# Conv + RWKV-7 + GLA trunk: two PSUM banks for the chain, three for small products, and a new order of the work around the chain

## The chip, the cores and the metric

The kernel runs on one core of a Trainium2 chip. The metric is the device time in microseconds. The kernel before took 1541.42, 1541.05 and 1535.45 us in three runs, median 1541.05.

## What is computed

A trunk of two layers over 128 context tokens and 512 noisy tokens (640 columns in the kernel), 1024 features, everything in float32. The first layer runs a short gated convolution and a bidirectional RWKV-7 recurrence on 16 heads of 64 side by side, the second layer bidirectional gated linear attention (GLA). The part that matters here is the recurrence of the first layer:

```python
u, gb, gc, zc, r, k, v, zw = jnp.split(h @ w_in, EVEN_SPLITS, axis=-1)
kk = heads(kf * k_k)
kk = kk / jnp.maximum(jnp.sqrt(jnp.sum(kk * kk, axis=-1, keepdims=True)), 1e-12)
def step(s, inp):                       # one token, state s of [value, key]
    r_t, w_t, k_t, kk_t, a_t, v_t = inp
    s_kk = jnp.einsum('zbhvk,zbhk->zbhv', s, kk_t)
    s = (s * w_t[..., None, :] - s_kk[..., :, None] * (kk_t * a_t)[..., None, :]
         + v_t[..., :, None] * k_t[..., None, :])
    return s, jnp.einsum('zbhvk,zbhk->zbhv', s, r_t)
```

## The kernel before

The recurrence is computed in chunks of 64 tokens: ten chunks in two directions d, for two heads at a time. Such a head pair is called hp (0 to 7). For each pair the products between the tokens of a chunk (the matrices G), the inverse of a triangular matrix made of them, and then a **chain** of eight steps are needed, in which the state X goes from chunk to chunk. The chain is serial, so its eight steps are cut into six **gaps** each, and the 48 gaps of a pair's **period** are filled with other work: the dense projections (blocks of 48 matmuls of 128x320, three products of split fp32r parts for each real one: r, v, k, zw of a pair and the units u, gc, gb, zc of the convolution), and **small work** that prepares the next pair.

The small work for pair hp+1 runs in period hp, in this order. `p_kb` scales the keys by the norms `rnb` (transposes into `prb`, VectorE product). `expand_all` makes the decayed operands ar and bk (VectorE and ScalarE, L733 to L766) and calls `pairs`, which forms the chunk products pG on TensorE and lets VectorE mask and evict them into G (L778). `inv_a` sends the diagonal blocks of G through DRAM (Ad) into the tile Ai, where a ladder of 60 VectorE operations inverts them (L845, L847), and back through DRAM (Td) into G. `inv_b` transposes them on VectorE (Tb, L868) and finishes the inverse with the products pT. `vrows`, `bonus`, `p_lr`, `p_kk` follow. `fin_b` and `fin_t` finish the pair before (normalised output oac, transposed into pgn, evicted by ScalarE into gn at L1061).

Orders are set in two ways. TensorE's instructions stay in the order in which the program writes them; this order comes from the class `Period`, which in each gap first runs the pieces of small work (`Work`) that are due by the table `PR`, and then as many pieces of dense work as a quota gives. On the other engines the scheduler goes by priorities: chain (CH) before evictions (EV), weight splits (SPL), preparation (PRE), finishing (FIN), background (BG). Each engine then runs its instructions strictly in the order written.

A chain step (`chain_step`) writes the products x and v into the bank pa; ScalarE copies them to rh (L958); two gaps; TensorE writes pu and adds to pa; ScalarE makes U from pa (L984); TensorE adds the products of U to pu; two gaps; VectorE makes the next state X from pu (L997). `bk_start` transposes the bk of the next step's chunks into the bank pbk, and ScalarE evicts them to bkt (L905). PSUM has eight banks: three for the dense blocks (psD), two in turn for small products (psM, function `pm`), and three for the chain (psC: pa, pu, pbk).

## Time and profile before

| What | us |
| --- | --- |
| Median of three runs | 1541.05 |
| The profiled execution | 1539.62 |
| its span | 1537.8 |
| setup, to the first dense matmul | 53.5 |
| preparation of pair 0 | 53.5 to 195.2 |
| periods 0 and 1 | 195.2 to 424.2 |
| periods 2 to 5, about 119.5 each | 424.2 to 902.5 |
| period 6 | 902.5 to 1014.5 |
| period 7, with the loads of the second layer | 1014.5 to 1141.2 |
| output projection and GLA layer | 1141.2 to 1537.8 |
| TensorE busy | 1362.7 (89%) |
| VectorE busy | 983.4 (64%) |
| ScalarE busy | 633.9 (41%) |
| GpSimd busy | 519.7 (34%) |

A stage starts where TensorE runs the first product of a pair's first chain step. Idle time of TensorE is listed by what released it: "pT <- DVE Tb" is time in which TensorE's next instruction writes pT and the last thing that it needed was VectorE's Tb. The granted clock tells at which share of its full speed TensorE was allowed to run; it has two levels, 1 (2.4 GHz) and 0.5 (1.2 GHz), and a mean between them is a mixture in time.

### The profile page before, as it was taken

The page shows a single profiled execution, that of the slowest core. Times are in us where ns is not written, and L with a number is a line of the kernel's source. Part 1 is how long each engine was busy: PE and PEld are TensorE (multiplying, and loading weights), DVE is VectorE, ACT ScalarE, POOL GpSimd, SP SyncE. Part 2 cuts the span into 40 slices and gives each one's busy share as a digit, 9 for nine tenths or more (in the row PEclk, how much of TensorE's full clock was granted, in tenths as well). Part 3 has the DMA queues.
Part 4 walks back from the last instruction along what each step waited for, and adds up shares of the span by engine and source line. Part 5 has one row for each costly group of instructions (what it writes and reads, how often), then busy time and mean ns, then how long its engine had stood idle before and what let it go on. Part 6 is the DMA issues. An engine that isn't in the chain of part 4 may idle for free. (4 is left out here: it accounts for less than half of the span.)

```text
span 1537.8 us, 34577 instructions
## 1 busy us (share of the span) xinstructions
PE 1362.7 (89%) x13495; PEld 1236.5 (80%) x13495; DVE 983.4 (64%) x2315; ACT 633.9 (41%) x1574; POOL 519.7 (34%) x675
## 2 busy tenths in 40 slices
PE   9689689589989989989998898789897999999997
PEld 4679678578878878878887887678887898999997
DVE  5285476486585595685675765766885668737554
ACT  4443253343443443443443353253235583444341
POOL 2333233123323232223323223144455534443332
PEclk9879899789989999999998998888998999999999
DMA  9012212112212212212212212236652332323233
GB/s 357 28 52 80 56 50 57 40 32 70 63 38 65 65 39 65 72 37 66 65 41 63 60 45 79 75 99 177 190 157 85 116 97 64 120 69 94 62 120 100
DMA packets 139636, 127.28 MB, mean 83 GB/s; under 512 B 54096, under 2 KB 121936, under 8 KB 139472
## 3 DMA queue, kind: packets, MB, share of 16 engines
q1 hardware_dynamic: 136912, 118.38, 25.9%
q0 software_dynamic: 2016, 6.16, 1.1%
...
q14 instruction: 58, 0.48, 0.1%
...
## 5 line engine op out<-in xcount | busy, mean ns | idle before, releaser
L130 PE MATMUL pG<-ar,bk 64*128 64x128 f32 x640 | 73.7, 336 | 39.5 <-ACT gn L1061 31.4
L847 DVE TENSOR_TENSOR Ai<-Ai 80x30 f32<-80x30 f32 (+14 forms) x240 | 100.6, 419 | 6.8
L845 DVE TENSOR_TENSOR Ai<-Ai 80x30 f32<-80x30 f32 (+14 forms) x240 | 94.6, 394 | 12.2 <-DMA Ai<-Ad 4.6
L130 PEld LDWEIGHTS pG<-ar,bk 64*128 64x128 f32 x640 | 56.3, 221 | 54.9 <-ACT gn L1061 33.7
L778 DVE TENSOR_TENSOR G<-pG,con 128x256 f32<-128x256 f32 (+1 forms) x128 | 57.8, 484 | 43.7 <-PE pG L130 42.9
L997 DVE SCALAR_TENSOR_TENSOR X<-pu,PC,XP 128x64 f32<-128x64 f32 x144 | 33.1, 274 | 62.6 <-POOL lo_zc L314 42.2
L228 DVE SCALAR_TENSOR_TENSOR gacc<-gw,cf,gacc 128x512 f32<-128x512 f32 x70 | 60.5, 909 | 11.9 <-DMA gw<-in_ada_dram 11.7
L952 POOL TENSOR_TENSOR XP<-X,PC 128x128 f32<-128x128 f32 (+2 forms) x56 | 29.1, 519 | 113.5 <-DVE X L997 80.8
L130 PE MATMUL pT<-Tb,G 32*32 32x32 f32 x640 | 17.5, 207 | 51.6 <-DVE Tb L868 51.6
L130 PEld LDWEIGHTS pT<-Tb,G 32*32 32x32 f32 x640 | 14.8, 121 | 55.4 <-issue 30.8
L677 DVE TENSOR_TENSOR_SCAN lw<-con,lw 128x320 f32<-128x320 f32 x32 | 28.8, 934 | 43.0 <-ACT lw L672 43.0
L314 POOL TENSOR_TENSOR lo_eoc<-wr_eoc,hi_eoc 128x256 fp32r<-128x256 f32 x48 | 44.3, 930 | 34.3 <-ACT hi_eoc L311 32.9
L130 PE MATMUL pd_r<-hi,hi_r 128*128 128x320 f32 x128 | 43.1, 337 | 11.5 <-ACT hi_r L311 11.5
L984 ACT ACTIVATE U<-pa 128x192 f32<-128x192 f32 (+1 forms) x64 | 19.3, 302 | 79.8 <-PE pa L130 78.8
L314 POOL TENSOR_TENSOR lo_gc<-wr_gc,hi_gc 128x256 fp32r<-128x256 f32 x32 | 25.9, 816 | 67.2 <-PE pd_r L130 43.5
L130 PE MATMUL pd_gc<-hi,lo_gc 128*128 128x320 f32 x128 | 47.8, 373 | 0.0
L1010 DVE SCALAR_TENSOR_TENSOR sz<-sz,pd_zw 128x320 f32<-128x320 f32 x16 | 7.7, 484 | 62.6 <-ACT sz L1009 62.6
L314 POOL TENSOR_TENSOR lo_gb<-wr_gb,hi_gb 128x256 fp32r<-128x256 f32 x32 | 26.3, 822 | 60.0 <-ACT hi_gb L311 59.6
L130 PE MATMUL pd_gc<-lo,hi_gc 128*128 128x320 f32 x128 | 45.8, 358 | 0.0
L130 PE MATMUL pd_gc<-hi,hi_gc 128*128 128x320 f32 x128 | 45.3, 354 | 0.0
L314 POOL TENSOR_TENSOR lo_zc<-wr_zc,hi_zc 128x256 fp32r<-128x256 f32 x32 | 23.8, 746 | 62.8 <-ACT hi_zc L311 61.8
L130 PE MATMUL pd_eoc<-hi,hi_eoc 128*128 128x320 f32 x128 | 44.4, 347 | 0.0
...
## 6 DMA issues: line engine op xcount, KB each, us to landing
...
```

Of the source, the lines that this page charges most:

```text
L130: tc.keep_in_program_order(T.matmul(*a, **kw))
L228: V.scalar_tensor_tensor(acc[j], w, c, acc[j], op0=ALU.mult, op1=ALU.add)
L314: le.tensor_tensor(lo, w, hi.bitcast(F32), op=ALU.subtract)
L677: V.tensor_tensor_scan(x, m, x, 0.0, op0=ALU.mult, op1=ALU.add)
L778: V.tensor_tensor(q["G"][h][:, d, c0 + a0:c0 + a0 + m], ps[h][:, 0:P * m].rearrange("p (c x) -> p c x", x=P), cc("mk", P, 256 * h + P * d) ...
L845: V.tensor_tensor(tt, Ai[:, 0:i, i:i + 1].to_broadcast([80, i, n]), Ai[:, i:i + 1, i + 1:].to_broadcast([80, i, n]), op=ALU.mult)
L847: V.tensor_tensor(Ai[:, 0:i, i + 1:], Ai[:, 0:i, i + 1:], tt, op=ALU.add)
L952: dict(V=V, G=G)[PR["xpc"]].tensor_tensor(XP[:, l0:nl], X[:, l0:nl], PC[:, s, l0:nl].unsqueeze(2).to_broadcast([P, nl - l0, 64]), op=ALU.mult)
L984: S.activation(U[:, 0:nl], pr[:, 0:nl], AF.Copy, scale=-1.0)
L997: V.scalar_tensor_tensor(Xn[:, l], po[:, 0, l], PC[:, s, l:l + 1], XP[:, l], op0=ALU.mult, op1=ALU.add)
L1010: V.scalar_tensor_tensor(sz[:, t], sz[:, t], 1.0, ps, op0=ALU.add, op1=ALU.mult)
```

## The change

- **Banks.** The chain holds pa and pu only. `bk_start` now stands after U, ahead of the products of U, and writes its transposes into columns 0 to 384 of pa, which U has just been read from. The bank pbk becomes the third in the turn of `pm`, from the end of the setup to the second layer's norm.
- **Chunk products in six units** of 4, 4 and 2 chunks for each direction, not eight of 3 and 2. A direction's four Ad transfers are issued as soon as its last unit is evicted; the layout of Ad and Td has the direction first.
- **Keys a period ahead.** `p_kb` of a pair runs at gaps 45 and 46 of the period before its preparation, not at gaps 0 to 2 of the preparation itself.
- **Order inside the gaps** (`Period`, "paired"): the first gap of each pair runs small work, then dense; the second dense, then small work. `inv_b` comes in two pieces, not four.
- **Priorities.** Small products' evictions run at the eviction priority (`evict`), `inv_a` just behind, `fin_s` behind that.
- **Table.** Convolution units after the change: 8 in the preparation of pair 0 (7 before), 4 in period 0 (1), 3 in each of periods 2 to 5 (4); one of the seven output blocks of period 7 moves behind the chain. The sum of the work stays. The expansion spreads over gaps 1 to 16 (5 to 14), `inv_a` is due at 17 (15), `inv_b` at 42 to 45 (40 to 44).
- **Weights.** The four weight blocks of the first dense block r0 are loaded and split during the setup.

The core of the diff follows; of the table it shows three entries. Left out are the eviction calls of the other small products, the allocation of PC, ar, bk and G (now in `expand_all`), the loop order of `inv_b`, and the planner's lines with the new pieces' numbers.

```diff
@@ table PR @@
- 'CN': [[1, 0, 0], [2, 1, 1], [2, 1, 1], [2, 1, 1], [2, 1, 1], [2, 1, 1], [2, 1, 1]],
+ 'CN': [[2, 1, 1], [2, 1, 1], [1, 1, 1], [1, 1, 1], [1, 1, 1], [1, 1, 1], [2, 1, 1]],
 ...
- 'ex': [5, 14],
- 'inv': 15,
+ 'ex': [1, 16],
+ 'inv': 17,
@@ -154,8 +159,22 @@
+    turn = [None]
     def pm(name):
+        if turn[0] is not None:
+            turn[0] += 1
+            if turn[0] % 3 == 2:
+                return psC.tile([P, 512], F32, tag="pbk", name=name)
         return psM.tile([P, 512], F32, tag="m", name=name)
+    def evict(f):
+        p = tc.cur_priority
+        prio(min(EV, p))
+        f()
+        prio(p)
@@ -523,6 +547,10 @@
+            prio(SPL)
+            for q in range(4):
+                ahead["r0", q] = weights(A["ew"][32], "r0", q)
+            prio(1)
@@ -559,6 +587,7 @@
+    turn[0] = 0
     st[0] = dict(k=et("k", "k0"), ok="k")
@@ -709,14 +739,8 @@
-            V.scalar_tensor_tensor(kk[:, u], k[:, u], pc("kk", hp), prb[:, 0:(t1 - t0) * P], op0=ALU.mult, op1=ALU.mult)
+            evict(lambda: V.scalar_tensor_tensor(kk[:, u], k[:, u], pc("kk", hp), prb[:, 0:(t1 - t0) * P], op0=ALU.mult, op1=ALU.mult))
@@ -765,34 +789,46 @@
-    def pairs(hp, d, c0, a0, m):
+    def pairs(hp, d, c0, m):
         q = st[hp]
-        bk, ar = q["bk"][:, d, c0:c0 + 5], q["ar"][:, d, c0:c0 + 5]
+        bk, ar = q["bk"][:, d, c0:c0 + m], q["ar"][:, d, c0:c0 + m]
+        ps = [pm(f"pG{hp}_{d}_{c0}_{h}") for h in range(2)]
         for i in range(m):
             for h in range(2):
-                mm(ps[h][:, P * i:P * i + P], bk[HS[h], a0 + i].rearrange("p a x -> p (a x)"),
-                   ar[HS[h], a0 + i].rearrange("p a x -> p (a x)"), start=True, stop=True)
-        for h in range(2):
-            V.tensor_tensor(q["G"][h][:, d, c0 + a0:c0 + a0 + m], ps[h][:, 0:P * m].rearrange("p (c x) -> p c x", x=P),
-                            cc("mk", P, 256 * h + P * d).unsqueeze(1).to_broadcast([P, m, P]), op=ALU.mult)
+                mm(ps[h][:, P * i:P * i + P], bk[HS[h], i].rearrange("p a x -> p (a x)"),
+                   ar[HS[h], i].rearrange("p a x -> p (a x)"), start=True, stop=True)
+        def ev():
+            for h in range(2):
+                V.tensor_tensor(q["G"][h][:, d, c0:c0 + m], ps[h][:, 0:P * m].rearrange("p (c x) -> p c x", x=P),
+                                cc("mk", P, 256 * h + P * d).unsqueeze(1).to_broadcast([P, m, P]), op=ALU.mult)
+        evict(ev)
 ...
-        quarters = [(d, c0) for d in range(2) for c0 in (0, 5)]
-        for x in quarters[:2]:
-            expand(hp, *x)
+        q = st[hp]
+        for c0 in (0, 5):
+            expand(hp, 0, c0)
-        for i, (d, c0) in enumerate(quarters):
-            pairs(hp, d, c0, 0, 3)
-            yield 520
-            pairs(hp, d, c0, 3, 2)
-            if i < 2:
-                expand(hp, *quarters[i + 2])
-            if i == 3:
-                st[hp]["ok"] += "g"
-            yield 520
+        for d in range(2):
+            for i, (c0, m) in enumerate(((0, 4), (4, 4), (8, 2))):
+                pairs(hp, d, c0, m)
+                if d == 0 and i < 2:
+                    expand(hp, 1, 5 * i)
+                if i == 2:
+                    for b in range(2):
+                        for h in range(2):
+                            r = 64 * (1 - h) + B * b
+                            nc.sync.dma_start(Ad[d, b, h].rearrange("c j t -> j c t"), st[hp]["G"][h][r:r + B, d, :, C + B * b:C + B * b + B])
+                    if d:
+                        st[hp]["ok"] += "g"
+                yield 210 * m
@@ -831,14 +870,9 @@
         Gt = st[hp]["G"]
-        for b in range(2):
-            for d in range(2):
-                for h in range(2):
-                    r = 64 * (1 - h) + B * b
-                    nc.sync.dma_start(Ad[b, d, h].rearrange("c j t -> j c t"), Gt[h][r:r + B, d, :, C + B * b:C + B * b + B])
-        nc.sync.dma_start(Ai, Ad.rearrange("b d h c j t -> (b d h c) j t"))
+        nc.sync.dma_start(Ai, Ad.rearrange("d b h c j t -> (d b h c) j t"))
         for i in range(1, B - 1):
@@ -891,13 +926,14 @@
-    def bk_start(hp, s):
+    def bk_start(hp, s, ta):
 ...
         q = st[hp]
-        pb = psC.tile([P, 3, P], F32, tag="pbk", name=f"pbk{hp}_{s}")
+        pb = ta[:, 0:384].rearrange("p (l x) -> p l x", x=P)
         for (l, d, c) in lanes:
             tr(pb[:, l], q["bk"][:, d, c].rearrange("p a x -> p (a x)"), ident)
@@ -926,12 +962,13 @@
+        ta, tu = (psC.tile([P, 512], F32, tag=t, name=f"{t}{hp}_{s}") for t in ("pa", "pu"))
+        pr = ta[:, 0:192].rearrange("p (l x) -> p l x", l=3)
+        po = tu[:, 0:384].rearrange("p (a l x) -> p a l x", a=2, l=3)
         if s == 0:
-            bk_start(hp, 0)
+            bk_start(hp, 0, ta)
-        pr = psC.tile([P, 3, 64], F32, tag="pa", name=f"pa{hp}_{s}")
-        po = psC.tile([P, 2, 3, 64], F32, tag="pu", name=f"pu{hp}_{s}")
@@ -988,6 +1024,7 @@
         def gu_mm(l, d, c, h):
             mm(po[HS[h], 1, l], Gt[h][HB[h], d, c, 0:C], U[HB[h], l], start=False, stop=l == nl - 1, skip_group_check=True)
+        bk_start(hp, s + 1, ta)
         each(bu_mm, upd)
         each(gu_mm, lanes)
@@ -1118,12 +1159,18 @@
-        def __call__(self):
+        def small(self):
             for m in self.misc:
                 m.upto(self.g)
-            self.credit += self.quota[self.g]
-            self.g += 1
-            if self.g == len(self.quota):
+        def __call__(self):
+            back = self.paired and self.g % 2
+            if not back:
+                self.small()
+            g = self.g
+            self.credit += self.quota[g]
+            if g + 1 == len(self.quota):
                 self.credit += 1e6
@@ -1132,6 +1179,9 @@
                     self.credit -= x
+            if back:
+                self.small()
+            self.g += 1
             prio(CH)
@@ -1226,17 +1276,19 @@
         if n < NHP:
-            misc += [Work(PRE, p_kb(n), 2, *PR["kb" + z], 270)]
+            if hp == 0:
+                misc += [Work(PRE, p_kb(1), 2, 0, 1, 270)]
             if hp == 0 and PR["lr1"]:
                 misc += [Work(PRE, p_lr(1), 9, *PR["lr1"], 270)]
-            misc += [Work(PRE, expand_all(n), 10, *PR["ex" + z], 540, (n, "r"))]
+            misc += [Work(PRE, expand_all(n), 8, *(PR["ex" + z] if hp else PR["ex0"]), 540, (n, "r"))]
+            iv = iv if hp else PR["inv0"]
 ...
             dense_ += [(FIN, p_z(hp)), *conv_next(c)]
@@ -1277,7 +1329,7 @@
         f.rest()
-        prio(FIN)
+        prio(EV + 600)
         run(fin_s(hp, 1 if hp == 7 else None))
@@ -1351,6 +1403,7 @@
     pss = psC.tile([P, 512], F32, tag="pa", name="pss1")
+    turn[0] = None
```

Three places show what moves. The first is TensorE in period 4, at the transposes pgn of pair 3's output between the chunk products pG of pair 5 (the last numbers tell tiles apart; pG5_0_0_3_0 is direction 0, chunks from 3 on, head 0). Before:

```order
L130 MATMUL pu4_1_8097<-U4_1_8253,G4_0_6456 64x64
L130 MATMUL pu4_1_8097<-U4_1_8253,G4_1_6457 64x64
L133 MATMUL pgn3_0_8267<-con_79,oac3_6074 128x128 x4
L130 MATMUL pG5_0_0_3_0_8276<-ar5_8009,bk5_8010 128x128
L130 MATMUL pG5_0_0_3_1_8277<-ar5_8009,bk5_8010 128x128
```

After:

```order
L135 MATMUL pd_v5_0_8481<-lo0_104,hi_v5_0_8459 128x320
L135 MATMUL pd_v5_0_8481<-hi0_103,lo_v5_0_8460 128x320
L138 MATMUL pgn3_0_8488<-con_79,oac3_6251 128x128 x4
L135 MATMUL pG5_1_4_0_8497<-ar5_8230,bk5_8231 128x128
L135 MATMUL pG5_1_4_1_8498<-ar5_8230,bk5_8231 128x128
```

Behind the transposes now comes the second unit of direction 1, not of direction 0, and a block of v ahead of them in place of the chain's products.

The second is VectorE in the same period, at the end of the ladder (Ai5), with the transposes Tb5 and the state X4_6 that the chain's next step reads. Before:

```order
L847 TENSOR_TENSOR Ai5_8529<-Ai5_8529 80x30
L1010 SCALAR_TENSOR_TENSOR sz4_9047<-sz4_9047,pd_zw4_0_9072 128x320
L997 SCALAR_TENSOR_TENSOR X4_6_9244<-pu4_6_9012,PC4_6453,XP4_6_9023 128x64 x3
L914 TENSOR_TENSOR oac4_7629<-pu4_6_9012,oac4_7629 128x2x64
L918 TENSOR_TENSOR oac4_7629<-pu4_6_9012,oac4_7629 128x64
L868 STREAM_TRANSPOSE Tb5_9153<-G5_0_8011 32x320
L868 STREAM_TRANSPOSE Tb5_9153<-G5_1_8012 32x320
```

After:

```order
L881 TENSOR_TENSOR Ai5_8592<-Ai5_8592 80x30
L1047 SCALAR_TENSOR_TENSOR sz4_9019<-sz4_9019,pd_zw4_0_9044 128x320
L900 STREAM_TRANSPOSE Tb5_9276<-G5_0_8232 32x320
L1034 SCALAR_TENSOR_TENSOR X4_6_9254<-pu4_6_9063,PC4_6772,XP4_6_9074 128x64 x3
L950 TENSOR_TENSOR oac4_7714<-pu4_6_9063,oac4_7714 128x2x64
L954 TENSOR_TENSOR oac4_7714<-pu4_6_9063,oac4_7714 128x64
L706 SCALAR_TENSOR_TENSOR lw6_9125<-con_79,lw6_9125 128x320
L900 STREAM_TRANSPOSE Tb5_9276<-G5_0_8232 32x320
L900 STREAM_TRANSPOSE Tb5_9276<-G5_1_8233 32x320
```

The first transpose has moved ahead of the state update, and scans of `p_lr` (lw6) stand between the others.

The third is TensorE at the start of period 4. Before, with the transposes in their own bank:

```order
L130 MATMUL pd_u5_1_7851<-hi0_103,lo_u5_3_7760 128x320
L133 MATMUL pbk4_0_7939<-con_79,bk4_6455 128x128 x3
L130 MATMUL pa4_0_7945<-X4_i_7626,ar4_6454 64x64 x4
L130 MATMUL pa4_0_7945<-V4_7316,G4_0_6456 64x64
L130 MATMUL pa4_0_7945<-V4_7316,G4_1_6457 64x64
```

After, in the bank pa4_0 itself:

```order
L135 MATMUL pd_gb5_1_7960<-hi0_103,lo_gb5_3_7761 128x320
L138 MATMUL pa4_0_8034<-con_79,bk4_6774 128x128 x3
L135 MATMUL pa4_0_8034<-X4_i_7711,ar4_6773 64x64 x4
L135 MATMUL pa4_0_8034<-V4_7359,G4_0_6775 64x64
L135 MATMUL pa4_0_8034<-V4_7359,G4_1_6776 64x64
```

The products of X4_i now write the bank that ScalarE reads the transposes from (bkt4_0).

## Rows read from the trace of the kernel before

**Rows 1.** The cores' answer: span, mean granted clock of TensorE (1 is full).

```profile
core 0: 1537.8 us, clock 0.932
```

**Rows 2.** Windows by stage: us, each engine's busy us (instructions), granted clock, DMA share, GB/s.

```profile
53.50:195.20 141.70, 111.70 (x841) 105.13 (x841) 81.54 (x186) 53.43 (x127) 48.72 (x61) 0.83 0.21 60
...
543.70:663.30 119.60, 106.97 (x1297) 96.20 (x1296) 78.89 (x208) 50.49 (x129) 36.51 (x51) 0.94 0.20 57
...
1141.20:1537.80 396.60, 365.37 (x2420) 351.69 (x2418) 241.05 (x521) 177.52 (x443) 161.50 (x206) 0.97 0.30 94
```

**Rows 3.** TensorE's waits, whole span: line, releaser, total us, times, longest us.

```profile
PE pT L130 <- DVE Tb L868: 51.6, 16, 13.1
PE pG L130 <- ACT gn L1061: 31.4, 12, 4.2
PE prb L133 <- DVE rnb L701: 15.3, 6, 3.8
PE pd_r L130 <- ACT hi_r L311: 11.5, 1, 11.5
PE pgn L133 <- DVE oac L1045: 10.6, 2, 9.6
PE pgn L133 <- DVE G L778: 6.5, 6, 1.2
PE pG L130 <- DVE G L778: 5.3, 3, 4.0
PE pa L130 <- DVE X L997: 4.0, 10, 1.1
```

**Rows 4.** Timeline around 568 us: start us, us, engine, what, idle before it.

```profile
568.13 0.66 PE L133 MATMUL pgn<-con,oac 128*128 128x128 f32 x4 [1.06 <-DVE G L778]
...
568.72 0.49 PE L130 MATMUL pG<-ar,bk 64*128 64x128 f32 x2
...
572.23 1.13 ACT L1061 ACTIVATE gn<-pgn,der 64x256 f32<-64x256 f32 x2
...
573.41 1.22 PE L130 MATMUL pG<-ar,bk 64*128 64x128 f32 x6 [4.20 <-ACT gn L1061]
```

**Rows 5.** Windows, TensorE alone, right after that wait: us, busy, granted clock.

```profile
569.58:579.82 10.24, 6.41 (x31) 0.50 0.15 50
```

**Rows 6.** Windows of the same period: expansion, and the inverse's ladder.

```profile
540.00:577.00 37.00, 29.37 (x343) 26.48 (x343) 33.66 (x95) 16.72 (x41) 12.16 (x16) 0.90 0.12 37
...
605.00:635.00 30.00, 29.79 (x338) 27.05 (x338) 28.03 (x74) 13.04 (x37) 10.22 (x16) 1.00 0.21 65
```

**Rows 7.** Timeline of VectorE: last eviction of G, ladder's ends, first transpose.

```profile
595.76 0.76 DVE L778 TENSOR_TENSOR G<-pG,con 128x256 f32<-128x256 f32 x2
...
605.01 0.18 DVE L845 TENSOR_TENSOR Ai<-Ai 80x30 f32<-80x30 f32 x1
...
634.76 0.21 DVE L847 TENSOR_TENSOR Ai<-Ai 80x30 f32<-80x30 f32 x1
...
639.56 2.21 DVE L868 STREAM_TRANSPOSE Tb<-G 32x320 f32<-32x320 f32 x4 [1.42 <-DMA G<-Td]
```

**Rows 8.** Groups by form, 543.7 to 663.3 us: VectorE's evictions of G.

```profile
L778 DVE TENSOR_TENSOR G<-pG,con 128x384 f32<-128x384 f32 x8 | 4.2, 551 | 4.4 <-PE pG L130 4.4
...
L778 DVE TENSOR_TENSOR G<-pG,con 128x256 f32<-128x256 f32 x8 | 3.1, 419 | 2.5 <-PE pG L130 2.4
```

**Rows 9.** The same view, TensorE: transposes for the state update.

```profile
L133 PE MATMUL pbk<-con,bk 128*128 128x128 f32 x19 | 4.0, 295 | 0.1
```

**Rows 10.** The same view, ScalarE: their eviction.

```profile
L905 ACT ACTIVATE bkt<-pbk 128x384 f32<-128x384 f32 x4 | 1.9, 485 | 0.3 <-PE pbk L133 0.3
```

**Rows 11.** Timeline of TensorE ahead of that transpose: dense products, then the chain's.

```profile
635.72 0.31 PE L130 MATMUL pd_zw<-hi,lo_zw 128*128 128x320 f32 x1
635.87 0.31 PE L130 MATMUL pd_zw<-hi,hi_zw 128*128 128x320 f32 x1
636.11 0.56 PE L130 MATMUL pu<-U,bkt 64*64 64x64 f32 x12
```

More of the change, by code (lines that the diff above doesn't have):

```diff
@@ L16 @@
  'pex': [4, 12],
+ 'ex0': [4, 15],
+ 'inv0': 16,
+ 'ib0': [44, 47],
+ 'lr0': [36, 43],
+ 'kk0': [42, 44],
  'pinv': 13,
@@ L27 @@
  'pinit': 30,
- 'ex': [5, 14],
- 'inv': 15,
- 'vr': 30,
- 'bo': [31, 33],
- 'lr': [36, 44],
- 'kk': [44, 47],
+ 'ex': [1, 16],
+ 'inv': 17,
+ 'vr': 26,
+ 'bo': [28, 30],
+ 'lr': [34, 41],
+ 'kk': [40, 42],
  'init': 40,
- 'fb': 7,
- 'ft': [10, 16],
- 'kb': [0, 2],
+ 'fb': 10,
+ 'ft': [13, 16],
+ 'kb': [45, 46],
  'al': 1.0,
@@ L67 @@
  'sh': 0.25,
- 'ex6': [5, 14],
- 'inv6': 15,
- 'vr6': 30,
- 'bo6': [31, 33],
+ 'ex6': [1, 16],
+ 'inv6': 17,
+ 'vr6': 26,
+ 'bo6': [28, 30],
  'init6': 43,
- 'fb6': 8,
- 'ft6': [11, 16],
- 'kb6': [0, 2],
+ 'fb6': 10,
+ 'ft6': [13, 16],
+ 'kb6': [2, 3],
  'base6': 3068,
- 'ld': [36, 44],
+ 'ld': [41, 44],
  'skip7': 0,
  'unit7': 1.35,
- 'noc': 7,
+ 'noc': 6,
  'lw7': 4,
@@ L320, in tile_trunk, with weights @@
     spl = [SPL]
+    ahead = {}
+    def weights(src, name, q, m=P):
+        w = wp.tile([P, 2, m], F32, tag="wraw", bufs=WR, name=f"wr_{name}_{q}")
+        nc.sync.dma_start(w, src[:, 2 * q:2 * q + 2])
+        return split(wp, w, "whi", "wlo", 6, f"{name}_{q}")
     def dense(src, name, evac, mov=h_of, m=P, after=None, qs=(0, 1, 2, 3)):
@@ L326, in dense @@
         for q in qs:
-            w = wp.tile([P, 2, m], F32, tag="wraw", bufs=WR, name=f"wr_{name}_{q}")
-            nc.sync.dma_start(w, src[:, 2 * q:2 * q + 2])
-            ws[q] = split(wp, w, "whi", "wlo", 6, f"{name}_{q}")
+            ws[q] = ahead.pop((name, q), None) or weights(src, name, q, m)
         prio(pr)
@@ new lines, in ev @@
+        def ev():
[3 more added lines that the diff above has]
+        evict(ev)
+    def expand_all(hp):
+        q = st[hp]
+        q["PC"] = wk.tile([P, 8, 3], F32, tag="PC", bufs=2, name=f"PC{hp}")
+        q["ar"] = wk.tile([P, 2, NCH, 2, C], F32, tag="ar", bufs=2, name=f"ar{hp}")
+        q["bk"] = wk.tile([P, 2, NCH, 2, C], F32, tag="bk", bufs=2, name=f"bk{hp}")
+        q["G"] = [wk.tile([P, 2, NCH, 2 * C], F32, tag=f"G{h}", bufs=2, name=f"G{hp}_{h}") for h in range(2)]
+        for c0 in (0, 5):
+            expand(hp, 0, c0)
+            yield 0
+        for d in range(2):
[11 more added lines that the diff above has]
+                yield 210 * m
@@ L807, in vrows, with ev @@
             pv = ps.rearrange("p (t h x) -> p t h x", t=4, h=2)
-            for h in range(2):
-                for r in range(2):
-                    S.activation(q["V"][HS[h], 2 * t0 + r:2 * t1:2], pv[HS[r], 0:t1 - t0, h], AF.Copy)
+            def ev():
+                for h in range(2):
+                    for r in range(2):
+                        S.activation(q["V"][HS[h], 2 * t0 + r:2 * t1:2], pv[HS[r], 0:t1 - t0, h], AF.Copy)
+            evict(ev)
         q["ok"] += "w"
@@ L1058, in fin_t, with ev @@
             pv = ps.rearrange("p (c x) -> p c x", x=P)
-            for h in range(2):
-                for i in range(2):
-                    S.activation(g3[HS[h], c0 + i:c0 + 2 * n:2], pv[HS[i], 0:n, 64 * h:64 * h + 64], AF.Identity,
-                                 scale=der[HS[h], 56 + hp:57 + hp], bias=der[HS[h], 64 + hp:65 + hp])
+            def ev():
+                for h in range(2):
+                    for i in range(2):
+                        S.activation(g3[HS[h], c0 + i:c0 + 2 * n:2], pv[HS[i], 0:n, 64 * h:64 * h + 64], AF.Identity,
+                                     scale=der[HS[h], 56 + hp:57 + hp], bias=der[HS[h], 64 + hp:65 + hp])
+            evict(ev)
             yield 430
@@ L1106, in tile_trunk, with __init__ @@
     class Period:
-        def __init__(self, dense_, misc, gaps, skip, unit, share={}, base=750, w=None):
+        def __init__(self, dense_, misc, gaps, skip, unit, share={}, base=750, w=None, paired=True):
+            self.paired = paired
             self.dense, self.misc, self.g, self.credit = list(dense_), misc, 0, 0
```

71 lines of the change are left out of this document (32 added, 39 removed).

## The prediction, made before the result was known

> **What bounds the kernel now.** I read the cores' answer first, then the stages, then what TensorE waits for, and only then the places. TensorE is busy in all stages and its granted clock is 0.932 in the mean [rows 1]: 2 x (1 - 0.932) x 1537.8 = 209 us of the span run at the lower of the two levels. In a steady period of 119.6 us TensorE is busy 106.97 us, VectorE 78.89 and ScalarE 50.49 [rows 2], so what can be won without less work is TensorE's idle time and its slow clock. The waits name it: eight entries make 51.6 + 31.4 + 15.3 + 11.5 + 10.6 + 6.5 + 5.3 + 4.0 = 136.2 us [rows 3], and nearly all lie before 1141 us, since the last stage of 396.6 us has TensorE busy for 365.37 at a clock of 0.97 [rows 2]. The dearest steady one is at 568 us: TensorE writes the transposes pgn at 568.13 and the first product of the next pG at 568.72, and then waits 4.20 us, until ScalarE has evicted the second half of pgn (572.23 to 573.36) [rows 4]. With two banks in turn the second head's pG needs the bank of pgn. The wait also costs clock: the 10.24 us from its middle on run at 0.50, with TensorE busy 6.41 us [rows 5], so about 3.2 us of work is lost, 0.31 of the stretch. Over the whole span 0.31 x 209 = 65 us. This is an estimate: some of those stretches hold more dense work, some less.
>
> **The waits, term by term.** The sum is made against the profiled execution (1539.6 us, 1.4 under the median).
>
> *pT on Tb, 51.6 us.* In a steady period the way from the last eviction of G (595.76, 0.76 us) over the DRAM trip to the ladder (605.01 to 634.97) and back to the transposes (639.56) is fixed at 43 us [rows 7], while VectorE is busy 28.03 of the ladder's 30.00 us [rows 6]. It shortens only if the ladder does, which doesn't change. The Ad transfers of direction 0 went out early before too. What changes is the cover: between the last pG and the first pT the order has 189 dense products (180 before), 160 chain records (140) and 16 transposes (14). At 0.15 us a dense product [rows 11], that is 1.3 us for those and under 1 us for the rest, some 2 us. Against it, VectorE now issues the first transpose ahead of the state update X_6 and scans between the others; of the four, pT needs a transpose for each head. So I leave 2 us of the five steady waits of 3.4, 10 us in all. The other 34.6 us lie in the preparation of pair 0 and periods 0 and 6, where dense blocks now stand in between (three more units in period 0, of 48 x 0.15 = 7 us each); I leave 9. Gain 33.
>
> *pG and pgn on evictions, 31.4 + 6.5 + 5.3 = 43.2 us.* With three banks pG no longer needs the bank of the pgn just written: the ScalarE entry goes. What is next late is VectorE. In the window of the expansion it is busy 33.66 of 37.00 us [rows 6], and twelve evictions in place of sixteen take off little: of 128x384 one takes 551 ns and of 128x256 419 ns [rows 8], so 128x512, which no row shows, comes by that step of 132 ns to about 0.68 us, and a pair's evictions fall from 7.8 to 8 x 0.68 + 4 x 0.42 = 7.1 us. (Its bounds are 0.55 and twice 0.42 us.) Moreover the order has only 47 dense products between the first and the last pG, where it had 67. So TensorE and VectorE run neck and neck there, and each unit waits somewhat: I take 4 us in each of six periods and 8 in the preparation of pair 0, 32 us. Gain 11, with bounds 0 and 35.
>
> *prb on rnb, 15.3 us.* The keys are scaled at gaps 45 and 46, behind the norms of gaps 40 to 42, with dense blocks between. I leave 1. Gain 14. *pd_r on hi_r, 11.5 us,* once: the weights are ready ahead, but low-rank products stand close behind, which need their own splits; between 0 and 11.5 I take half. Gain 6. *pgn on oac, 10.6 us,* behind the chain: an output block of 7 us or more now runs there. Gain 9. *pa on X, 4.0 us:* the transpose ahead of X_6 can cost here; I add 2.
>
> *A new wait.* At each period's start the bk transposes go into pa, and the products of X_i directly behind them write the same bank. They must wait for the last transpose (0.295 us [rows 9]) and ScalarE's eviction (0.485 us [rows 10]), on top of whatever ScalarE is at: 0.8 to 1.5 us, I take 1.0, eight times. Loss 8. In the other steps two gaps of dense work lie between that eviction and the next product, and I cost them at nothing; without that cover it would be 0.8 us a step.
>
> *The rest.* A change from dense to chain products starts 0.24 us after the last one, not 0.15 [rows 11]; by the order a steady period has 75 changes of kind, not 86, some 1 us less. For the periods with such an order: gain 6. The moved convolution units, the output block and the bank turn for them carry no time of their own, since TensorE's work stays the same in all.
>
> **The sum.** Waits: 33 + 11 + 14 + 6 + 9 - 2 - 8 = 63 us of 136. The slow clock follows the waits: 65 x 63/136 = 30. With the 6 that is 99 us: 1539.6 - 99 = 1440.6, and 1.4 more for the median, 1442 us, a little over 6% less. About 0.5%, 8 us, is what a measurement can tell from no change.
>
> **What the Trainium skill says.** VectorE left 1.42 us idle ahead of the first transpose, which waited for the transfer of G [rows 7]. The Trainium skill, page "PSUM — Partial Sum Buffer", section "Engine vs sequencer instructions", says that VectorE's queue is strictly first in, first out; by that X_6, now behind a transpose, waits as long as the transfer does, and the first rival gains weight. The trace agrees as far as it goes: nothing ran in those 1.42 us. The same page's section on bank collisions has software keep two engines off one bank at a time; that speaks against putting the transposes into pa, and by it the third rival holds for each step.
>
> **The rivals.**
>
> *The inverse's trip becomes the bound.* It takes 43 us, whatever TensorE does [rows 7]. If periods shrink more around it than I think, or X_6 waits behind the transpose, 4 us more are waited in each of six periods, and each such wait brings a slow stretch like that of rows 5 (3.2 us): 6 x 7.2 = 43, so 1485. For it: VectorE's order. Against it: nine dense products more as cover. Chance 0.17.
>
> *The third bank buys nothing,* because the wait for gn is only followed by one of the same length for G. Then the 11 us and their share of clock, 5, go: 1458. For it: VectorE 33.66 of 37.00 us [rows 6]. Against it: in rows 4 the bank, not VectorE, was last. Chance 0.12.
>
> *The chain turns serial.* If the transposes and their eviction are waited for in every step, 3 x 0.295 + 0.485 = 1.37 us [rows 9, 10] in 64 steps is 88 us, of which 8 are in my sum: 1522. It decides once the two gaps behind U hold less than that. Chance 0.05.
>
> *Slower: the expansion runs at half clock.* Place: the third of a period with the chunk products. If each of the six units waits for two evictions and an expansion step ahead of them on VectorE, 2 x 0.68 + 0.5 and a little, say 2.2 us, TensorE has such a pause every few us and the 37 us run at 0.50, which loses 0.31 x 37 = 11.5. A period then has 13.2 + 11.5 there in place of my 4 + 2.5: 18 us more, seven times (with the preparation of pair 0) 127: 1569. It is slower than before from 1.7 us a unit on. For it: the preparation of pair 0 already runs at a clock of 0.83 [rows 2]. Against it: three banks let a unit begin before the last one is evicted. Chance 0.06.
>
> *More goes than I grant.* If the expansion's waits and Tb's steady ones vanish too, 27 us of waits and 12 of clock: 1403. Chance 0.12. My forecast, 1425 to 1465, keeps 0.48.
>
> **Range and chances.** From 1402 to 1490 it holds the forecast, the first two rivals and the last but for some of their edges, about 0.8. Faster 0.91, the same 0.03, slower 0.06.
>
> **What would show it.** In the profile after: the entry of pG on ScalarE's gn gone and pG on VectorE's G at some 30 us; prb under 2; pT near 19; a new wait of about 1 us at each period's first chain product; steady periods of 103 to 107 us (7 of the difference is moved work); the mean clock near 0.95. I am wrong if the waits for pT or for X grow, if VectorE's evictions hold each unit of pG, or if the steps wait for the transposes in pa.

## The result, and the profile after

The changed kernel took 1466.72 us in the median of four runs (1463.09 to 1472.39), the kernel before 1540.87 beside it: a ratio of 0.953 with a 95% interval of 0.949 to 0.957. That is 74 us less where 99 were forecast; it lies inside the range, 25 us above the forecast. The profiled execution took 1467.22 us, its span is 1465.5 and its mean granted clock 0.944 (0.932 before, [rows 1]).

First the page's row of all engines (busy us, share of the span, instructions; PE is TensorE, PEld its weight loads, DVE VectorE, ACT ScalarE, POOL GpSimd), then windows by stage as in [rows 2]: us, busy us of TensorE, its weight loads, VectorE, ScalarE and GpSimd, granted clock, DMA share, GB/s. They are the preparation of pair 0, period 3, period 7, and everything behind the chain.

```profile
PE 1353.6 (92%) x13495; PEld 1240.8 (85%) x13495; DVE 981.3 (67%) x2283; ACT 630.8 (43%) x1574; POOL 519.3 (35%) x675
```

```profile
53.50:193.40 139.90, 119.21 (x895) 111.68 (x894) 83.47 (x183) 54.23 (x130) 49.66 (x63) 0.89 0.23 65
...
521.80:629.80 108.00, 100.15 (x1244) 91.36 (x1243) 75.28 (x197) 47.87 (x121) 33.63 (x46) 0.92 0.20 56
...
938.80:1062.30 123.50, 112.75 (x1077) 104.16 (x1078) 84.83 (x134) 43.94 (x106) 53.04 (x56) 0.85 0.55 164
1062.30:1465.50 403.20, 377.68 (x2492) 363.98 (x2490) 246.54 (x527) 179.22 (x449) 165.64 (x211) 0.97 0.31 96
```

TensorE's idle time, span less busy time, went from 1537.8 - 1362.7 = 175.1 to 1465.5 - 1353.6 = 111.9 us: 63.2 less. Its busy time fell by only 9.1 us. Period 3 took 108.0 us (119.6 before, with one unit of 7 us more), periods 2 to 5 together 422.3 (478.3 before, with four units more). Period 7 is the odd one: 123.5 us at a clock of 0.85, though a block of the output projection has left it.

The waits of TensorE after, in the columns of [rows 3]:

```profile
PE pG L135 <- DVE G L804: 15.3, 8, 3.4
PE pG L135 <- DVE bk L790: 12.2, 13, 2.0
PE pgn L138 <- DVE oac L1082: 8.6, 3, 4.4
PE pa L135 <- ACT bkt L941: 6.4, 8, 1.1
PE pss L135 <- ACT lw L697: 6.1, 3, 3.7
PE pT L135 <- DVE Tb L900: 6.0, 9, 3.1
PE pa L135 <- DVE X L1034: 5.4, 7, 1.3
...
PE plr_ta L135 <- ACT w2h L672: 5.2, 1, 5.2
```

The entry of pG on ScalarE's gn (31.4 us) is gone, that of prb (15.3) too, and pT on Tb fell from 51.6 to 6.0 (3.6 more wait for small steps of VectorE that now stand among the transposes). New are pa on bkt, eight waits of together 6.4 us, and pss on ScalarE's lw.

The clock tells the other half. The windows are all stretches at 0.50: us, TensorE's busy us, granted clock, DMA share, GB/s, and their sum. Of the kernel before:

```profile
1153.26:1166.91 13.65, 5.46 (x21) 0.50 0.27 74
...
sum 212.54, PE 139.11; mean PE 5.80
```

Of the changed kernel:

```profile
440.81:444.23 3.42, 3.42 (x14) 0.50 0.03 10
...
604.65:618.31 13.66, 12.63 (x139) 0.50 0.28 64
...
1034.73:1048.38 13.65, 13.65 (x71) 0.50 0.56 161
...
sum 166.50, PE 146.13; mean PE 6.09
```

Before, a long wait lay within the slow stretch: in the 13.65 us at 1153 TensorE was busy for 5.46. After, the stretches are shorter in sum (166.5 us, not 212.5) but full: at 1034 all 13.65 us are work. If work takes twice its time at half speed, the loss is half of the busy time: 139.11/2 = 69.6 us before, 146.13/2 = 73.1 after. This is an estimate, and rather a high one, since dense products at 0.50 are 0.26 us apart in place of 0.15 (shown below). By it the loss did not fall. Differences of a few us in it are no more than executions differ by: the mean granted clock of the four runs of the changed kernel lay between 0.940 and 0.950.

The chain of work that ended last, as the profile follows it back from the last instruction, can't be compared between these two: of the kernel before it reaches back only to 940 us, into period 6 (VectorE has 8% there, but all shares together are 39%). It is followed nearly to the start in the kernel that has the old order and only the banks changed (e6 below). That one by engine and by line, shares of the span:

```profile
PE 50%; DVE 31%; DMA 10%; issue 4%; ACT 3%; POOL 2%; SPq 0%; DVEq 0%; POOLq 0%; ACTq 0%
DVE Ai L854 5%; DVE Ai L852 4%; DMA gw<-in_ada_dram 4%; PE pu L130 3%; PE pd_gb L130 3%; PE pd_v L130 3%; PE pd_r L130 3%; PE pd_oo L130 3%; PE pd_zg L130 3%; PE pd_zw L130 3%; PE pG L130 3%; PE pd_qk L130 2%; PE pa L130 2%; PE pd_u L130 2%; PE pd_vg L130 2%
```

The changed kernel:

```profile
PE 45%; DVE 34%; DMA 7%; issue 4%; POOL 3%; ACT 2%; SPq 0%; DVEq 0%; POOLq 0%; ACTq 0%
DVE Ai L881 6%; DVE Ai L879 6%; PE pd_oo L135 3%; PE pd_zg L135 3%; PE pu L135 3%; PE pd_eoc L135 3%; PE pd_gb L135 3%; PE pd_r L135 3%; DVE bk L790 3%; PE pd_v L135 3%; PE pd_qk L135 2%; PE pd_vg L135 2%; DVE bk L787 2%; DMA gw<-in_ada_dram 2%; PE pd_u L135 2%
```

VectorE has 31% in the old order and 34% in the new, the ladder Ai 9% and 12%. The inverse's trip lay on the chain in the old order too, and still does; what fell is TensorE's wait for its end, 51.6 us at pT before.

### The profile page after: what moved, and what is told of

It is laid out like the page before. It is cut to its first block, busy times and chain, and to the rows that moved or that the text cites. A ratio compares the mean times of both kernels' runs of the same rounds, so it can differ in the third digit from the quotient of the medians.

```text
span 1465.5 us, 34615 instructions
## 1 busy us (share of the span) xinstructions
PE 1353.6 (92%) x13495; PEld 1240.8 (85%) x13495; DVE 981.3 (67%) x2283; ACT 630.8 (43%) x1574; POOL 519.3 (35%) x675
## 3 DMA queue, kind: packets, MB, share of 16 engines
q1 hardware_dynamic: 136912, 118.38, 27.3%
## 4 chain that ended last, share of the span: by engine, by line
PE 45%; DVE 34%; DMA 7%; issue 4%; POOL 3%; ACT 2%; SPq 0%; DVEq 0%; POOLq 0%; ACTq 0%
DVE Ai L881 6%; DVE Ai L879 6%; PE pd_oo L135 3%; PE pd_zg L135 3%; PE pu L135 3%; PE pd_eoc L135 3%; PE pd_gb L135 3%; PE pd_r L135 3%; DVE bk L790 3%; PE pd_v L135 3%; PE pd_qk L135 2%; PE pd_vg L135 2%; DVE bk L787 2%; DMA gw<-in_ada_dram 2%; PE pd_u L135 2%
## 5 line engine op out<-in xcount | busy, mean ns | idle before, releaser
L135 PE MATMUL pG<-ar,bk 64*128 64x128 f32 x640 | 66.4, 320 | 27.7 <-DVE G L804 15.3
L135 PEld LDWEIGHTS pG<-ar,bk 64*128 64x128 f32 x640 | 52.3, 212 | 40.4 <-DVE G L804 17.2
L804 DVE TENSOR_TENSOR G<-pG,con 128x512 f32<-128x512 f32 (+1 forms) x96 | 53.1, 594 | 26.1 <-PE pG L135 25.8
L247 DVE SCALAR_TENSOR_TENSOR gacc<-gw,cf,gacc 128x512 f32<-128x512 f32 x70 | 59.9, 895 | 15.3 <-DMA gw<-in_ada_dram 15.1
L333 POOL TENSOR_TENSOR lo_eoc<-wr_eoc,hi_eoc 128x256 fp32r<-128x256 f32 x48 | 40.2, 846 | 50.9 <-ACT hi_eoc L330 30.9
L333 POOL TENSOR_TENSOR lo_r<-wr_r,hi_r 128x256 fp32r<-128x256 f32 x32 | 25.2, 791 | 82.0 <-ACT hi_r L330 81.4
L994 ACT ACTIVATE rh<-pa 128x192 f32<-128x192 f32 (+1 forms) x64 | 19.2, 300 | 65.5 <-PE pa L135 65.5
L135 PE MATMUL pd_eoc<-hi,lo_eoc 128*128 128x320 f32 x128 | 44.0, 343 | 2.5 <-POOL lo_eoc L333 2.5
L790 DVE TENSOR_TENSOR bk<-ta,iP 64x320 f32<-64x320 f32 x64 | 44.4, 693 | 1.4
L135 PE MATMUL pd_gb<-hi,hi_gb 128*128 128x320 f32 x128 | 43.4, 339 | 0.7 <-DVE cy L619 0.7
L135 PE MATMUL pd_eoc<-lo,hi_eoc 128*128 128x320 f32 x128 | 43.4, 339 | 0.4 <-POOL lo L1207 0.4
L135 PE MATMUL pd_gb<-hi,lo_gb 128*128 128x320 f32 x128 | 42.4, 331 | 0.0
```

Of the source, the lines that this page charges most:

```text
L135: tc.keep_in_program_order(T.matmul(*a, **kw))
L247: V.scalar_tensor_tensor(acc[j], w, c, acc[j], op0=ALU.mult, op1=ALU.add)
L333: le.tensor_tensor(lo, w, hi.bitcast(F32), op=ALU.subtract)
L790: E(2).tensor_tensor(bk[HS[h], :, h], ta3[HS[h]], iP3[HS[h]], op=ALU.mult)
L804: V.tensor_tensor(q["G"][h][:, d, c0:c0 + m], ps[h][:, 0:P * m].rearrange("p (c x) -> p c x", x=P), cc("mk", P, 256 * h + P * d).unsqueeze ...
L994: S.activation(rh[:, 0:nl], pr[:, 0:nl], AF.Copy)
```

## The experiments

All times are medians, each beside the kernel before on the same chip (1541.15 to 1541.63 us there). Idle time is span less TensorE's busy time.

### The third bank undone (e1)

```diff
-    turn[0] = 0
+    turn[0] = None
```

> The changed kernel with the third bank left idle: small products turn over two banks again. Theory (the bank carried the waits of pG and pgn): the products of a unit wait for ScalarE's eviction of pgn and for VectorE's of the unit before, some 4 to 5 us in each of six periods; idle time of TensorE up by 25 to 35 us, time 1490 to 1500 us (changed kernel 1467). Rival (the eviction priority alone cured them): within 5 us of 1467.

Measured: 1511.23 us (1509.18 to 1513.49), 44.5 more than the changed kernel. TensorE's waits:

```profile
PE pG L135 <- DVE G L804: 25.4, 10, 7.4
PE pG L135 <- ACT gn L1100: 20.8, 12, 2.7
PE plr_lw L135 <- ACT lw L697: 16.1, 5, 5.4
```

Idle time is 145.8 us, 33.9 more, as the theory had it. The waits for gn are back (20.8), those of pG for G grew by 10 us, and a third entry came that nobody had asked for: the low-rank products wait for ScalarE's lw, 16.1 us. The rival falls: priorities alone don't cure these waits. The time lies above the theory's 1490 to 1500 because TensorE's busy time rose too, by 8.0 us to 1361.6, at a mean clock of 0.940 (0.944 in the changed kernel's profile).

### The banks alone (e6)

The kernel before with the chain in two banks, bk's transposes in pa, and the third bank in the turn of small products.

```diff
-        pb = psC.tile([P, 3, P], F32, tag="pbk", name=f"pbk{hp}_{s}")
+        pb = ta[:, 0:384].rearrange("p (l x) -> p l x", x=P)
...
+    turn[0] = 0
```

> The kernel before with nothing but the banks changed: chain in two banks, transposes of bk in pa behind U, third bank in the turn of small products. Theory: the waits of pG for ScalarE's gn (31.4 us) go or fall to a third, eight waits of 0.8 at the periods' starts come, pT and prb stay: 1515 to 1528 us (before 1541). Rival (the order and the priorities made the gain, the bank none): 1537 to 1550.

Measured: 1535.72 us (1528.8 to 1540.83), a ratio of 0.9961 (0.9942 to 0.9981): 6 us, less than the theory's 13 at least, more than the rival's none. The waits:

```profile
PE pT L130 <- DVE Tb L875: 54.5, 16, 13.1
PE pG L130 <- DVE G L785: 16.4, 14, 3.4
...
PE pa L130 <- DVE X L1005: 10.3, 6, 3.7
PE pa L130 <- ACT bkt L912: 8.5, 8, 2.2
...
PE pG L130 <- ACT gn L1069: 6.0, 4, 2.7
```

The bank did what was expected of it: gn fell from 31.4 to 6.0. But pG on G rose from 5.3 to 16.4, pa on X from 4.0 to 10.3, and the move of bk costs 8.5. With the old order the third bank changes the name of the waits and little else. The Trainium skill, page "Perfetto Trace Analysis", section "Matmuls", has independent groups of matmuls turn through different banks, so that one is evicted under the next; this run shows that in the old order the turn is worth 0.4%.

### Eight units of chunk products, three banks (e8)

```diff
-            for i, (c0, m) in enumerate(((0, 4), (4, 4), (8, 2))):
+            for i, (c0, m) in enumerate(((0, 3), (3, 2), (5, 3), (8, 2))):
```

> The changed kernel with the chunk products in eight units of 3 and 2 chunks again, three banks kept. Theory (with three banks a unit of two banks may begin before the last one is evicted, whatever its size; sixteen evictions take 0.6 us more a period, and the last comes a gap or two later): 1466 to 1476 us. Rival (the six larger units made the gain, and the third bank was needed only for them): 1485 or more.

Measured: 1509.98 us (1509.45 to 1511.03), 43 more. The theory falls, the rival's time fits: with the rest of the change in place, undoing the larger units costs as much as undoing the bank. The new order without both was not run, so whether the two losses add up is not shown. The waits, then period 3, VectorE's last eviction and first ladder step in it, and the same of the changed kernel with the ladder's last step and the first transpose:

```profile
PE pG L135 <- DVE G L804: 25.9, 11, 5.3
PE pss L135 <- ACT lw L697: 20.8, 4, 6.2
```

```profile
538.20:653.30 115.10, 99.96 (x1244) 90.72 (x1243) 77.25 (x201) 47.38 (x121) 35.90 (x46) 0.93 0.20 53
```

```profile
581.01 0.75 DVE L804 TENSOR_TENSOR G<-pG,con 128x256 f32<-128x256 f32 x2
...
593.66 0.19 DVE L879 TENSOR_TENSOR Ai<-Ai 80x30 f32<-80x30 f32 x1 [1.89 <-DMA Ai<-Ad]
```

```profile
559.18 0.76 DVE L804 TENSOR_TENSOR G<-pG,con 128x256 f32<-128x256 f32 x2 [3.43 <-PE pG L135]
...
570.25 0.19 DVE L879 TENSOR_TENSOR Ai<-Ai 80x30 f32<-80x30 f32 x1 [1.46 <-DMA Ai<-Ad]
...
600.32 0.21 DVE L881 TENSOR_TENSOR Ai<-Ai 80x30 f32<-80x30 f32 x1
...
607.43 0.50 DVE L900 STREAM_TRANSPOSE Tb<-G 32x320 f32<-32x320 f32 x1
```

In the changed kernel G is done 559.18 + 0.76 - 521.8 = 38.1 us after the period's start; in the kernel before it was 596.52 - 543.7 = 52.8 [rows 7]; with eight units 581.76 - 538.2 = 43.6. From there the trip takes 10 us to the ladder, 30 for the ladder and 7 to the first transpose; before it took 8.5, 30 and 4.6 [rows 7]. A later G therefore moves everything behind it. And a wait that I hadn't seen grows: ScalarE's low-rank step writes the buffer that the ladder's tile holds (both are tagged "lw", in one buffer). In the changed kernel:

```profile
603.85 0.53 ACT L697 ACTIVATE lw<-plr_lw,der 128x320 f32<-128x320 f32 x1 [4.94 <-DMA Td<-Ai]
604.28 0.27 ACT L941 ACTIVATE bkt<-pa 128x128 f32<-128x128 f32 x1
```

```profile
604.43 0.42 PE L135 MATMUL pss<-con,kk 128*128 128x2 f32 x2 [3.70 <-ACT lw L697]
...
605.13 0.47 PE L135 MATMUL pd_zw<-lo,hi_zw 128*128 128x320 f32 x1
605.39 0.47 PE L135 MATMUL pd_zw<-hi,lo_zw 128*128 128x320 f32 x1
```

ScalarE stood idle for 4.94 us until the transfer Td had read the ladder's tile. TensorE's norms stood behind it for 3.70 us, and the dense products that were 0.15 us apart [rows 11] are 0.26 us apart afterwards: the 13.66 us from 604.65 on run at 0.50. ScalarE's queue is strictly first in, first out by the Trainium skill (page "PSUM — Partial Sum Buffer", section "Engine vs sequencer instructions"); the trace agrees: the eviction bkt, whose transpose TensorE had run at 598.69, came only behind the waiting step, at 604.28. With eight units this entry is 20.8 us (6.1 in the changed kernel), in the run with two banks 16.1. Idle time is 142.7 us, 30.8 more; TensorE's busy time is 1365.0, 11.4 more.

### Low-rank products and norms two gaps later (e4)

```diff
- 'lr': [34, 41],
+ 'lr': [36, 43],
- 'kk': [40, 42],
+ 'kk': [42, 44],
```

> The changed kernel with the low-rank products of the next pair at gaps 36 to 43 (not 34 to 41) and the norms at 42 to 44 (not 40 to 42). In the changed kernel ScalarE stood 4.9 us in period 3 until the inverse's transfer had freed the buffer that the next low-rank result takes; TensorE waited 3.7 us for it, and 13.65 us ran at half clock behind that. Theory (a short wait costs mostly by the clock behind it): the 6.1 us of such waits and 5 to 8 us of clock go, 1452 to 1457 us. Rival (only the wait counts): 1460 to 1462. Second rival (the wait comes back at pT): 1467.

Measured: 1481.61 us (1473.86 to 1484.73), 15 more, worse than all three expectations. The waits for lw are gone, but:

```profile
PE pa L135 <- DVE X L1034: 13.6, 10, 2.3
...
PE pT L135 <- DVE Tb L900: 11.5, 12, 3.0
```

pa on X has risen from 5.4 to 13.6 and pT on Tb from 6.0 to 11.5. Two of the longest waits for X, 2.17 us in period 2 and 2.01 in period 3, lie within the ladder; in period 2 VectorE ran a ladder step just ahead of the state update X that TensorE waited for:

```profile
492.68 0.36 DVE L879 TENSOR_TENSOR Ai<-Ai 80x198 f32<-80x198 f32 x1
...
493.38 0.45 PE L135 MATMUL pa<-X,ar 64*64 64x64 f32 x8 [2.17 <-DVE X L1034]
```

Idle time is 118.7 us, only 7 more. The larger part is TensorE's busy time, 1364.2 (1353.6), at a mean clock of 0.933 (0.944); the profiled execution, 1484.73 us, is the slowest of the five. Why the clock fell more often is open. In the kernel before, the table had the low-rank products at gaps 36 to 44 and the norms at 44 to 47; the change had moved both ahead, to where they meet the end of the ladder.

### The convolution units where they were (e7)

```diff
-PR = {'NC0': 8,
- 'CN': [[2, 1, 1], [2, 1, 1], [1, 1, 1], [1, 1, 1], [1, 1, 1], [1, 1, 1], [2, 1, 1]],
+PR = {'NC0': 7,
+ 'CN': [[1, 0, 0], [2, 1, 1], [2, 1, 1], [2, 1, 1], [2, 1, 1], [2, 1, 1], [2, 1, 1]],
```

> The changed kernel with the convolution units where the kernel before had them: 7 in the preparation of pair 0, 1 in period 0, 4 in each of periods 2 to 5. Theory (three units in period 0 were cover for the inverse's trip there): period 0 waits 8 to 13 us for Tb again with a slow stretch behind it, the rest only moves; 1475 to 1485 us. Rival (where the units stand makes no difference, the work is the same): 1462 to 1471.

Measured: 1465.79 us (1457.75 to 1467.62): no difference. Windows of period 0 and period 3:

```profile
191.60:295.90 104.30, 89.66 (x1168) 80.62 (x1169) 74.34 (x189) 45.97 (x118) 26.36 (x38) 0.92 0.18 49
516.50:626.10 109.60, 103.21 (x1297) 93.84 (x1296) 81.57 (x203) 49.99 (x128) 37.00 (x50) 0.98 0.22 62
```

Period 3 holds a unit more than in the changed kernel and takes 109.6 us in place of 108.0, at a clock of 0.98 in place of 0.92; period 0 holds three units less and takes 104.3 in place of 112.9. Periods 2 to 5 together took 435.7 us (406.8 to 842.5), in the changed kernel 422.3 (419.7 to 842.0): 13 us for four units, 28 us of work. The theory's wait did not come: in period 0 pT does not wait for Tb. A wait of 8.7 us for it stands in the preparation of pair 0, which has a unit less, and in period 0 TensorE waits 5.1 us at pss for lw. Idle time is 121.4 us, 9.5 more than in the changed kernel, and busy time 9.2 less, at a mean clock of 0.953 in place of 0.944. So more waiting was made up by a faster clock. Why the clock fell less often with the same work is open, and what a unit in a steady period is worth can't be read from this run.

### Keys back, and gaps unpaired (e2, e3)

```diff
-            if hp == 0:
-                misc += [Work(PRE, p_kb(1), 2, 0, 1, 270)]
+            misc += [Work(PRE, p_kb(n), 2, 0, 1, 270)]
```

> The changed kernel with the keys scaled at gaps 0 and 1 of the preparation again, not at gaps 45 and 46 of the period before. Theory (the step ahead removed the wait of prb and lets the expansion begin at once): prb waits 2 to 3 us in six periods, the expansion and with it the first chunk products come later, 1482 to 1497 us (changed kernel 1467). Rival (the wait was hidden behind others anyway): up to 1472.

Measured: 1480.33 us (1478.2 to 1482.97), 13.6 more, just under the theory's range; the rival falls. But not by the theory's wait: prb isn't in the list. It shows up behind the expansion: in its list of waits pgn on oac is 14.2 us (8.6 in the changed kernel), pG on G 19.8 (15.3) and pa on X 9.4 (5.4). Idle time is 132.3 us, 20 more, and busy time 9.5 less.

```diff
-        def __init__(self, dense_, misc, gaps, skip, unit, share={}, base=750, w=None, paired=True):
+        def __init__(self, dense_, misc, gaps, skip, unit, share={}, base=750, w=None, paired=False):
```

> The changed kernel with small work at the front of every gap, as before the change. Theory (the waits went by banks, cover and the earlier keys; the side of a gap on which small work stands matters little): 1461 to 1473 us. Rival (the order in a pair of gaps is what gives each unit of pG time to be evicted): more waits of pG for G, 1480 or more.

Measured: 1485.01 us (1474.93 to 1485.31), 18 more. The theory (no matter) falls. In its profiled execution, of 1474.93 us, idle time is 121.7 us, 10 more, spread over many entries; the rival's larger wait of pG for G is 17.2 us there (15.3), so its mechanism isn't shown either. A part can be counted: in periods 0 to 6 TensorE goes 488 times from a dense product (one that writes a tile pd) to another kind or back, in the changed kernel 378 times and in the kernel before 522 times. At 0.24 - 0.15 = 0.09 us a change [rows 11], 110 more make 10 us, an estimate. The rest of the 18 us stays open.

### What one wait costs (e9, e10)

ScalarE evicts the first bk transposes of each period three or six times over, so that a known wait between dense work gets longer.

```diff
-        S.activation(bt[:, u], pb[:, u], AF.Copy)
+        for _ in range(3 if s == 0 else 1):
+            S.activation(bt[:, u], pb[:, u], AF.Copy)
```

> The changed kernel with ScalarE's eviction of the first transposes of each period done three times over, so that the first chain product, which waits for it, waits about 1.0 us longer at eight places; nothing else waits on it directly. It prices one wait of about 1.8 us between dense work. If a wait costs only its length: 8 us more, 1475. If TensorE's clock falls behind each such wait and the dense work behind it runs at half clock for some 3.4 us: 8 x (1.0 + 1.7) = 22 more, 1488.

> The same with the eviction six times over: the wait is about 2.4 us longer, some 3.2 us in all, at eight places. If a wait costs only its length: 19 us more, 1486. If the clock falls behind each for 3.4 us of dense work: 33 more, 1500; if it falls for 6.8 us: 46 more, 1513.

Measured: 1483.89 us (1478.85 to 1488.89) with three, 1507.34 (1505.47 to 1508.78) with six, 17 and 41 more. With three, two of the eight waits on the timeline, and the stretches behind them:

```profile
528.57 0.45 PE L135 MATMUL pa<-X_i,ar 64*64 64x64 f32 x8 [3.26 <-ACT bkt L942]
```

```profile
751.69 0.45 PE L135 MATMUL pa<-X_i,ar 64*64 64x64 f32 x8 [2.41 <-ACT bkt L942]
```

```profile
529.05:532.46 3.41, 3.41 (x23) 0.50 0.26 101
...
751.69:755.10 3.41, 3.41 (x45) 1.00 0.07 20
```

With six, the sum of the waits, and two of the stretches at or in them:

```profile
PE pa L135 <- ACT bkt L942: 33.7, 8, 5.2
```

```profile
195.22:198.63 3.41, 3.41 (x28) 0.50 0.00 0
...
427.33:434.16 6.83, 4.73 (x33) 0.50 0.01 2
```

Waits of 1.83, 2.06, 2.31 and 2.41 us were followed by full clock; one of 2.04, at the start of period 7, was not. All eleven of 3.18 us and more had a stretch at 0.50 of 3.4 or 6.8 us behind or around them. So with six the waits grew from 6.4 to 33.7 us, by 27.3, and the time by 41: a factor of 1.5. With three they grew by more than planned, 6.4 to 20.7, and the time by 17: a factor of 1.2, or 0.8 to 1.6 over its four runs.

### Two tries for better, and the one that was (e5, e11, e12)

```diff
-            bk_start(hp, 0, ta)
+            bk_start(hp, 0, pm(f"pbk{hp}_0"))
```

> The changed kernel with the first transposes of bk of each period in a bank of the small products, so that the first chain product no longer writes the bank that ScalarE reads. Theory: the eight waits on that eviction (6.4 us together, 0.6 to 1.1 each) go and nothing else changes, since the clock never fell behind them: 1459 to 1462 us. Rival (the bank's turn shifts and pG waits in its place): 1465 to 1472.

Measured: 1460.25 us (1457.62 to 1464.19), a ratio to the kernel before of 0.947 (0.945 to 0.949). The time is as the theory had it, the way there is not. The page's row:

```profile
PE 1344.3 (92%) x13495; PEld 1233.7 (85%) x13495; DVE 979.1 (67%) x2283; ACT 631.0 (43%) x1574; POOL 520.2 (36%) x675
```

The eight waits on bkt are gone, but idle time is 1457.7 - 1344.3 = 113.4 us, 1.5 more than in the changed kernel: waits of a like size stand elsewhere (pa on X 7.4, pT on Tb 7.3, pG on G and bk 29.4). The profiled execution is shorter by 9.3 us of busy time, at a mean clock of 0.950 (0.944). It is the best version that was run; its interval touches that of the changed kernel (0.949 to 0.957).

On top of it, with the output's transposes (e12), or with them and the norms (e11), a gap later:

```diff
- 'ft': [13, 16],
+ 'ft': [14, 17],
- 'kk': [40, 42],
+ 'kk': [41, 43],
```

> The changed kernel with the first transposes of bk in a bank of the small products (1460 us by itself), the output's transposes pgn a gap later (14 to 17) and the norms a gap later (41 to 43). Theory: the waits of pgn for oac (6.4 us) and of pss for the low-rank step (5.5 us) fall by half and a slow stretch or two with them: 1448 to 1456 us. Rival (they come back at pT and X, as with the low-rank products moved): 1460 to 1475.

> As the run before it, but only the output's transposes moved, the norms as in the changed kernel. Theory: the waits of pgn for oac (6.4 us in three periods, one of 4.4) mostly go: 1452 to 1457 us. Rival (pG stands later in exchange): 1460 to 1468.

Measured: 1475.72 us (1474.72 to 1480.52) for both, 1470.58 (1460.59 to 1476.24) for the output alone: worse by 15 and 10 than the run they build on. In the first of them the waits moved as in e4: pT on Tb is 19.2 us, pG on bk 17.4, pa on X 10.8. The waits of pss for lw are gone there, those of pgn for oac are down to 1.1. With the output alone pgn on oac is 2.7 and pG on G and bk 39.2, where the run below it has 6.4 and 29.4. Both theories fall. The rivals' mechanisms show, and both times lie just above the rivals' ranges; the six runs of the output alone spread over 16 us.

## Why the prediction was right, and where not

**The waits.** The forecast left 73 us of the listed waits, and TensorE's idle time fell by 63.2 us, as forecast. That the two agree to a microsecond is luck, since the terms missed in both directions. Term by term, what was left: pT 9.6 with the small steps (19 forecast), pG on G and bk 27.5 (32; the 12.2 for bk, VectorE's expansion, had been 2.8 before and no entry of the forecast), prb none (1), the low-rank wait at the start 5.2 (6), pa on X 5.4 (6), the new wait on bkt 6.4 (8). Two terms were wrong and happened to be small: pgn on oac is 8.6, not 1.6, since it left the place behind the chain and came up within three periods (a longest of 4.4 us); and pss on lw, 6.1, was not foreseen. The eviction of 128x512, which no row of before showed, was put at 0.68 us:

```profile
L804 DVE TENSOR_TENSOR G<-pG,con 128x512 f32<-128x512 f32 x8 | 5.1, 680 | 0.1
```

**The slow clock is the step that failed.** Its level was right: 65 us were estimated, 69.6 is the sum over all stretches. Its fall was not: I let it go in proportion to the waits, 30 us less, and by the same estimate it rose by 3.5. The share of 0.31 was taken from a stretch that held a long wait and then scaled by the waits; but the waits that went had lain in slow stretches and had covered the slow clock there (73 of 212 us), and those that stayed are followed by dense work at half speed (20 of 166 us are idle; 8 and 9 us of the two lie at the program's end). That is read off the two traces; no run takes such a wait away alone. Two runs show that the length of the idle time does not set the clock: e4 and e7 are idle for 118.7 and 121.4 us, and by their mean clocks of 0.933 and 0.953 they ran 199 and 138 us at half clock. Waits that are added do cost clock: in e9 and e10 0.2 and 0.5 us for each us of wait, in e1 and e8 8.0 and 11.4 us of busy time for 33.9 and 30.8 us of idle time. The forecast's 65/136 = 0.48 is the upper end of that. So the price of an added wait was not far off; that all the waits taken away would give it back was wrong. What in the new order took it again is open. The term is mis-sized by 33 us, more than the whole miss of 27 us in the profiled execution (99 against 72.4).

**The small term** makes up the other 6 us. TensorE's work at full speed, busy time less the estimated loss, is some 13 us less, not 6. The forecast counted 11 fewer changes of kind in a steady period; between dense products and others the traces have 54 where 76 were, and over periods 0 to 6 144 fewer. At 0.09 us that is 13 us, an estimate. The run without paired gaps (e3), with 110 changes more, agrees: its busy time of 1351.5 us, less half of the 121.6 us of it that lie at 0.50, is 10 us above the changed kernel's.

**The rivals.** *The inverse's trip* did not become dearer: pT waits 6.0 us for Tb where it waited 51.6, and another 6.1 us is waited at lw's buffer, which the rival did not name. e1, e7 and e8 run into that buffer, e4 into pT. The nine products of cover that the forecast counted on are low-rank ones: between the last pG and the first pT of period 3 stand 171 dense products (172 before) and 16 low-rank ones (6 before), and the results of eight of these need the ladder's buffer. *The third bank buys nothing* was right of the bank in the old order (0.4%) and wrong in the new one (44 us). *The chain turns serial* did not happen: pa waits for bkt at the eight period starts alone. There it waits 0.6 to 1.1 us; the two gaps covered it in the other steps. The rule of the Trainium skill (page "PSUM — Partial Sum Buffer", section "PSUM bank collisions raise a hardware error") has software keep two engines off one bank. No run here shows it apart: the products of X_i write columns of pa that the transposes hold, and would have to wait without the rule too. *Half clock over the whole expansion* did not happen: the longest wait of pG is 3.4 us, and period 3 as a whole ran at 0.92. That X_6 stood behind a transpose cost nothing that the trace shows: pa on X went from 4.0 to 5.4 us in all.

**Period 7,** 123.5 us at 0.85, took 126.7 before, with the output block of 7 us or more that has left it. Its three slow stretches hold 37.6 us, where two held 23.9. Why the clock fell more often there is open.
